# Two small steps of a two-layer encoder kernel moved: the exponent of the cumulative decays, and its negative

## The chip, the cores and the metric

The kernel runs on one core of a Trainium2 chip. The metric is device time in microseconds (us) of one execution, given as the median of several runs. The engines are named as the profile names them: PE (TensorE matmul), PEld (TensorE weight load), DVE (VectorE), ACT (ScalarE), POOL (GpSimd) and SP (SyncE, which here only issues DMAs).

## The reference, cut to what matters

Two residual layers over 256 tokens of width 1024. Each layer makes one wide projection and runs two token mixers side by side: a gated delta rule in both directions, and a differential softmax attention. The gated delta rule, in its chunked form:

```python
g = jnp.cumsum(g.reshape(bsz, nh, nc, CHUNK), axis=-1)
gdiff = g[..., :, None] - g[..., None, :]
decay = jnp.where(lower, jnp.exp(jnp.where(lower, gdiff, 0.0)), 0.0)
L = jnp.where(strict, jnp.einsum('bhncd,bhnmd->bhncm', kb, k) * decay, 0.0)
T = triangular_solve(eye + L, eye)
u, w = T @ vb, T @ (kb * jnp.exp(g)[..., None])
# per chunk, in order:
v_new = u_c - w_c @ state
o = (q_c * jnp.exp(g_c)[..., None]) @ state + qk_c @ v_new
```

What the change is about is `exp(g)`: the exponent of the cumulative log decays. In the kernel it is the tile `E_` (128 x 32: two directions by two chunks by eight heads), and `nE` is its negative. `E_` scales the second term of the output, `nE` the correction of the second chunk's values.

## The kernel before, in words

The kernel uses chunks of 128 tokens, so a layer has two per direction. All matmuls of the projections take operands split in a high and a low part (`hi_...`, `lo_...`): ACT casts the high part of a 256-row piece of weights (`weights`, line 308), DVE subtracts it from the raw weights to get the low part (line 310), and PE makes three products with them (`proj_tm`, lines 324, 325 and 326: high by high, high by low, low by high). High and low tiles have two buffers each, raw tiles three. Four such pieces make a projection; PE goes from one to the next without any other work between, so a piece that is late makes PE wait.

A layer begins with the value projections of the attention (`pp_vb`), and the k projections of the delta rule (`pf_k`), followed by the convolution of k. In `conv` each block of channels is convolved with five taps: ACT makes the middle tap out of PSUM (line 675, `cvk`, `cvq`, `cvv`), DVE adds the four others (line 679), ACT makes a tanh (line 685, `thk`, `thq`), and DVE multiplies (line 690, which for q and k writes `kq`). Then come the q projections of the delta rule (`pf_q`), in two halves, and between them the first q projection of the attention (`pp_qk`).

`gates()` is written after the k convolutions. It makes the log decays, sums them with a matmul, turns them (`gcps`), and writes `ngc`, the negative of the cumulative log decays (line 776), then `E_` with ACT's Exp (line 777) and `nE` with DVE (line 778). `log_decays()` takes the sums of squares of k, and among others their logarithm with ACT's Ln (line 742, in place on a part of the tile that order calls `ge`); `lnc` (lines 744 to 746) is made of it. `decays` raises the decay tiles `B` with ACT, `weigh_k` sums them (line 824, `dsum`) and multiplies the sum with the gram matrix of k into `A` (line 825, four times in a layer), and `turn_blocks()` comes behind it; its first step is an Exp of the small tile `kds` (line 843).

`E_` is first read by line 1015, and `nE` by line 1005, in `chunks`, long after the projections around which they are made.

The order on each engine is decided at build time: a scheduler places each instruction by what it needs and by its own estimates. `tc.high_priority(offset=HP)` lets an instruction go as early as it can, and `behind(x)` places one behind the instruction x. Ahead of some activations, where the function changes, the build puts an `ACT_TABLE_LOAD` on ACT. The program has 11 rows of that kind, before and after the change.

Of the kernel before, what the change touches and what calls it, by code (L numbers as in the profile page):

```python
# [11 lines left out]
AF = mybir.ActivationFunctionType  # L12
ALU = mybir.AluOpType
# [15 lines left out]
HP = None  # L29
# [20 lines left out]
def hybrid_encoder(  # L50
# [19 lines left out]
    V, S, G, T = nc.vector, nc.scalar, nc.gpsimd, nc.tensor  # L70
# [15 lines left out]
    def bank(name):  # L86
        return ps_m.tile([P, 512], F32, tag="m", name=name)
# [10 lines left out]
    def mid(ap, n):  # L98
        return ap.unsqueeze(1).to_broadcast([ap.shape[0], n] + list(ap.shape[1:]))
# [4 lines left out]
    mark = {}  # L104
# [44 lines left out]
    def heads4(ap):  # L149
        return ap.rearrange("p (h e) -> p h e", e=P)  # L150
# [119 lines left out]
    def behind(ins):  # L270
        return nullcontext() if ins is None else tc.issue_after(ins)
# [235 lines left out]
    for l in range(DEPTH):  # L507
# [223 lines left out]
        nE = small.tile([P, 4, NH], F32, tag="nE", name=f"nE{l}")  # L731
        ngc = small.tile([P, 4, NH], F32, tag="ngc", name=f"ngc{l}")
        E_ = small.tile([P, 4, NH], F32, tag="E_", name=f"E_{l}")

        def log_decays():
            kss = e_[:, :, 32:40]
            V.tensor_scalar(kss, ssk, 4.0 * EPS, None, ALU.add)
            kh = small.tile([P, NM, NH], F32, tag="kh", name=f"kh{l}")
            V.tensor_scalar(kh, kss, 1.0 / 16.0, None, ALU.mult)
            G.tensor_tensor(nrm.rearrange("p m h -> p (m h)"), kh.rearrange("p m h -> p (m h)"),  # L740
                            phalf, ALU.pow)
            S.activation(kss, kss, AF.Ln)
            for d in range(2):
                V.scalar_tensor_tensor(lnc[:, d], ev[:, :, d * 8 : d * 8 + 8], -1.0, kss,
                                       ALU.mult, ALU.subtract)
            V.tensor_tensor(lnc.rearrange("p d c h -> p (d c) h"), lnc.rearrange("p d c h -> p (d c) h"),
                            ngc, ALU.add)
# [6 lines left out]
        def gates():  # L754
            with behind(mark[f"k{l}1", 0][0]):
                S.activation(ev, ev, AF.Ln)
            V.scalar_tensor_tensor(ev, a_, 0.0, ev, ALU.max, ALU.add)
            glog = small.tile([P, NM, 16], F32, tag="glog", name=f"glog{l}")
            V.tensor_tensor(glog, ev[:, :, 16:32], mid(nega, NM), ALU.mult)

            gr_ps = bank(f"grps{l}")
            for d in range(2):
                for c in range(NM):
                    dc = 2 * d + c
                    T.matmul(gr_ps[0:8, dc * P : (dc + 1) * P], glog[:, c, d * 8 : d * 8 + 8],
                             tri[:, d, :], start=True, stop=True)
            grow = work.tile([8, 4, P], F32, tag="w2c", name=f"grow{l}", bufs=3)
            with behind(mark[f"k{l}1", 3][1]):
                V.tensor_copy(grow.rearrange("h c i -> h (c i)"), gr_ps[0:8, :])
            gv = gdr.rearrange("c h d i -> h d c i")  # L770
            for d in range(2):
                G.dma_start(out=gv[:, d], in_=grow[:, 2 * d : 2 * d + 2])
            gc_ps = bank(f"gcps{l}")
            for dc in range(4):
                T.transpose(gc_ps[:, dc * 8 : dc * 8 + 8], grow[:, dc, :], ident[:8, :8])
            V.tensor_scalar(ngc, gc_ps[:, :32].rearrange("p (c h) -> p c h", c=4), -1.0, None, ALU.mult)
            S.activation(E_, ngc, AF.Exp, scale=-1.0)
            V.tensor_scalar(nE, E_, -1.0, None, ALU.mult)


        A = big.tile([P, 2, NM, 4, P], F32, tag="A", name=f"A{l}")
# [3 lines left out]
        def gram(nm, g, c, slot, after=None):  # L785
            gp = (bank if slot else bank_c)(f"{nm}{l}{g}{c}")
            for j4 in range(4):
                kqh = kq[:, 4 * g + j4, c]
                with behind(after):
                    mark[nm, g, c] = T.matmul(gp[:, j4 * P : (j4 + 1) * P], kqh[:, 0, :], kqh[:, slot, :],  # L790
                                              start=True, stop=True).ins
            return heads4(gp)
# [28 lines left out]
        def weigh_k(g, c):  # L821
            dec = B[:, c, 4 * g : 4 * g + 4].rearrange("p h d i -> p d h i")
            dsum = work.tile([P, 4, P], F32, tag="w2c", name=f"dsum{l}{g}{c}", bufs=3)
            V.tensor_tensor(dsum, dec[:, 0], dec[:, 1], ALU.add)
            V.tensor_tensor(A[:, g, c], gram("kk", g, c, 0), dsum, ALU.mult)

        def weigh_q(g, c, after):
            bv = B[:, c, 4 * g : 4 * g + 4]
# [12 lines left out]

        def turn_blocks():
            S.activation(kds, kds, AF.Exp)
            Av = A.rearrange("p g c h i -> p (g c h) i")
            for b in range(4):
                G.dma_start(out=adr[b].rearrange("t j i -> j t i"), in_=Av[blk(b), :, blk(b)])
            adv = adr.rearrange("b t j i -> (b t) j i")
            G.dma_start(out=la[0:64], in_=adv)
            G.dma_start(out=lt[64:P], in_=adv)
            G.memset(X, 0.0)  # L850
            G.memset(X.rearrange("p c i -> p (c i)")[:, 0:1024:33], 1.0)
# [268 lines left out]
        with tc.high_priority(offset=HP):  # L1120
            gates()
# [7 lines left out]
        lambdas()  # L1129
        spread()  # L1130
        log_decays()
        conv("q", C_QA, 1, 0)
        qk_part(0, 0)
        cut = mark["qkT", 0]
        decays(0, 0)
        weigh_k(0, 0)
        decays(0, 1)
        weigh_k(0, 1)
        decays(1, 0)
        weigh_k(1, 0)  # L1140
        decays(1, 1)
        weigh_k(1, 1)
        turn_blocks()
        conv("q", C_QA, 1, 1)
        take_blocks()
# [237 lines left out]
```

## Time and profile before

| | |
|---|---|
| median of 3 runs | 751.39 us (750.81 to 751.85) |
| the profiled execution | 751.43 us, of which the profile spans 749.7 us |
| granted TensorE clock, mean | 0.997 |
| PE busy | 739.6 us, 99% of the span |
| PEld busy | 641.2 us, 86% |
| DVE busy | 586.4 us, 78% |
| ACT busy | 480.9 us, 64% |
| POOL busy | 139.0 us, 19% |

PE is busy nearly all of the time. A row of a timeline gives the start, the time that the instruction was busy, engine, line, operation, the tile written and the tiles read, and in brackets how long the engine had been idle and who ended it. Consecutive instructions overlap by a little, so the distance between two starts is shorter than what one is busy.

### The profile page before, as it was taken

What the parts mean: (1) busy time and instruction counts of PE and PEld (TensorE: products, weight loads), DVE (VectorE), ACT (ScalarE), POOL (GpSimd) and SP (SyncE); (2) the same over time, 40 slices, a digit from 0 to 9 for tenths busy, and PEclk for the clock granted to TensorE, in tenths of its full rate; (3) what the DMA queues carried; (4) which work ended last, traced back from release to release, by engine and by line L of the source; (5) the groups of instructions that cost most, each with busy time, mean ns of one, the idle gap of its engine ahead of it and who ended that gap; (6) DMA issues with size and microseconds to landing.
All of it is one profiled execution on the core that took longest, in us unless ns stands there. A gap on an engine that the chain in (4) does not pass through costs nothing.

```text
span 749.7 us, 13916 instructions
## 1 busy us (share of the span) xinstructions
PE 739.6 (99%) x5176; PEld 641.2 (86%) x5176; DVE 586.4 (78%) x1109; ACT 480.9 (64%) x1022; POOL 139.0 (19%) x221
## 2 busy tenths in 40 slices
PE   8999999999999999999999999999999999999996
PEld 6999899987888889888889889889778888998885
DVE  8696898999985965578667769999999669537782
ACT  6657775667876576645456578555787757566552
POOL 5004111112022440100000150202110425301000
PEclk9999999999999999999999999999999999999998
DMA  8755566776666462567674466767666747336641
GB/s 260 238 169 169 167 171 199 212 209 198 208 182 177 151 181 84 170 199 245 202 232 134 130 189 174 216 178 233 199 171 194 197 129 234 94 114 200 218 143 57
DMA packets 73734, 135.46 MB, mean 181 GB/s; under 512 B 12944, under 2 KB 13921, under 8 KB 73666
## 3 DMA queue, kind: packets, MB, share of 16 engines
q1 hardware_dynamic: 64750, 113.65, 50.3%
q0 software_dynamic: 7936, 19.35, 8.8%
q10 hardware_dynamic: 980, 1.58, 0.6%
q8 instruction: 41, 0.67, 0.4%
q14 instruction: 27, 0.22, 0.1%
HBM read 125.53 MB, written 9.01 MB: 179 GB/s over the span
## 4 chain that ended last, share of the span: by engine, by line
PE 95%; DVE 1%; issue 1%; ACT 1%; DMA 1%; SPq 0%; POOLq 0%; POOL 0%; DVEq 0%; ACTq 0%
PE pp_vb L369 4%; PE pp_qk L325 4%; PE pp_qk L326 3%; PE pp_qk L324 3%; PE sc L1060 2%; PE pp_o L369 2%; PE pf_k L385 2%; PE pp_za L325 2%; PE pf_v L385 2%; PE pf_v L389 2%; PE pp_gb L324 2%; PE pp_gb L325 2%; PE pp_zb L324 2%; PE pf_q L387 2%; PE pf_k L387 2%; PE pf_v L387 2%
## 5 line engine op out<-in xcount | busy, mean ns | idle before, releaser
L325 PE MATMUL pp_qk<-lo_qk,hT 128*128 128x512 f32 x128 | 50.5, 395 | 1.1 <-DVE lo_qk L310 1.1
L326 PE MATMUL pp_qk<-hi_qk,hT 128*128 128x512 f32 x128 | 49.9, 390 | 0.0
L310 DVE TENSOR_TENSOR lo_qk<-raw_qk,hi_qk 128x1024 fp32r<-128x1024 f32 x32 | 39.0, 1220 | 11.8 <-ACT hi_qk L308 11.6
L324 PE MATMUL pp_qk<-hi_qk,hT 128*128 128x512 f32 x128 | 45.4, 395 | 0.0
L308 ACT CAST hi_qk<-raw_qk 128x1024 fp32r<-128x1024 f32 x28 | 29.4, 1049 | 22.9 <-PE pp_qk L326 7.1
L1070 ACT ACTIVATE es<-sc,mx 128x256 f32<-128x256 f32 x64 | 29.6, 474 | 19.6 <-DVE mx L1068 19.6
L310 DVE TENSOR_TENSOR lo_pb<-raw_pb,hi_pb 128x1024 fp32r<-128x1024 f32 x16 | 19.6, 1224 | 21.2 <-ACT hi_pb L308 20.9
L387 PE MATMUL pf_q<-hT,hi_q 128*128 128x256 f32 x128 | 36.1, 286 | 0.0
L385 PE MATMUL pf_k<-hT,hi_k 128*128 128x256 f32 x128 | 36.0, 287 | 0.0
L385 PE MATMUL pf_v<-hT,hi_v 128*128 128x256 f32 x128 | 35.8, 285 | 0.0
L387 PE MATMUL pf_v<-hT,hi_v 128*128 128x256 f32 x128 | 35.8, 284 | 0.0
L385 PE MATMUL pf_q<-hT,hi_q 128*128 128x256 f32 x128 | 35.8, 284 | 0.0
L387 PE MATMUL pf_k<-hT,hi_k 128*128 128x256 f32 x128 | 35.7, 283 | 0.0
L389 PE MATMUL pf_q<-hT,lo_q 128*128 128x256 f32 x128 | 35.1, 287 | 0.0
L389 PE MATMUL pf_v<-hT,lo_v 128*128 128x256 f32 x128 | 34.5, 287 | 0.0
L389 PE MATMUL pf_k<-hT,lo_k 128*128 128x256 f32 x128 | 34.3, 283 | 0.0
L308 ACT CAST hi_pa<-raw_pa 128x1024 fp32r<-128x1024 f32 x16 | 16.9, 1055 | 22.2 <-PE pp_pa L326 16.0
L679 DVE SCALAR_TENSOR_TENSOR cvq<-pf_q,cw,cvq 128x254 f32<-128x254 f32 (+1 forms) x64 | 29.9, 477 | 0.9 <-ACT cvq L675 0.2
L325 PEld LDWEIGHTS pp_qk<-lo_qk,hT 128*128 128x128 f32 x128 | 24.0, 188 | 7.4 <-DVE lo_qk L310 2.4
L679 DVE SCALAR_TENSOR_TENSOR cvv<-pf_v,cw,cvv 128x254 f32<-128x254 f32 (+1 forms) x64 | 29.7, 474 | 0.1
L679 DVE SCALAR_TENSOR_TENSOR cvk<-pf_k,cw,cvk 128x254 f32<-128x254 f32 (+1 forms) x64 | 29.0, 477 | 1.0 <-ACT cvk L675 0.2
L310 DVE TENSOR_TENSOR lo_pa<-raw_pa,hi_pa 128x1024 fp32r<-128x1024 f32 x16 | 19.6, 1224 | 11.2 <-ACT hi_pa L308 11.2
(414 smaller groups left out, 2536.9 us busy)
## 6 DMA issues: line engine op xcount, KB each, us to landing
raw_qk<-in_w_in_dram SPq DMA_DIRECT2D x32, 512.0 KB, 3.8
raw_k<-in_w_in_dram SPq DMA_DIRECT2D x16, 512.0 KB, 4.5
raw_q<-in_w_in_dram SPq DMA_DIRECT2D x16, 512.0 KB, 3.7
raw_v<-in_w_in_dram SPq DMA_DIRECT2D x16, 512.0 KB, 3.8
raw_zb<-in_w_in_dram SPq DMA_DIRECT2D x16, 512.0 KB, 3.7
raw_za<-in_w_in_dram SPq DMA_DIRECT2D x16, 512.0 KB, 3.7
raw_ga<-in_w_in_dram SPq DMA_DIRECT2D x16, 512.0 KB, 4.7
raw_pb<-in_w_pb_dram SPq DMA_DIRECT2D x16, 512.0 KB, 3.9
```

What stands on the lines that cost most here:

```text
L308: high = (V.tensor_copy if kp in turned else S.copy)(hi[:, :, :n], raw[:, :, :n]).ins
L310: mark[nm, kp] = high, V.tensor_tensor(lo[:, :, :n], raw[:, :, :n], hi[:, :, :n].bitcast(F32), ALU.subtract).ins
L324: T.matmul(o, act[kt // 4][:, 0, kt % 4, ts_], hi, start=kt == 0, stop=False)
L325: T.matmul(o, act[kt // 4][:, 0, kt % 4, ts_], lo, start=False, stop=False)
L326: mark["proj"] = T.matmul(o, act[kt // 4][:, 1, kt % 4, ts_], hi, start=False, stop=kt == KT - 1).ins
L369: mark["proj"] = T.matmul(o, act[kt // 4][:, pa, kt % 4, ts_], ws[kt][1 + pw], start=kt == 0 and n_ == 0, stop=kt == KT - 1 and n_ == 2).ins
L385: T.matmul(o, hi[:, cs], act[kt // 4][:, 0, kt % 4, :], start=first, stop=False, skip_group_check=True)
L387: T.matmul(o, hi[:, cs], act[kt // 4][:, 1, kt % 4, :], start=False, stop=False, skip_group_check=True)
L389: T.matmul(o, lo[:, cs], act[kt // 4][:, 0, kt % 4, :], start=False, stop=done, skip_group_check=True)
L679: V.scalar_tensor_tensor(ca[:, o0:o1], acc[:, b, o0 + sft : o1 + sft], cw[:, j, cb : cb + 1], ca[:, o0:o1], ALU.mult, ALU.add)
L1060: mm = T.matmul(sp[n][:, qt * SEQ : (qt + 1) * SEQ], qkT[h // 4][rows, 0, h % 4, qt * P : (qt + 1) * P], qkT[h // 4][rows, 1, h % 4, :], s ...
L1070: S.activation(es[:, n, qt, :], spv[:, qt, :], AF.Exp, bias=mx[:, n, qt : qt + 1], accum_out=s_all[:, h, n, qt : qt + 1])
```

## The change

Two edits. The Exp that makes `E_` leaves `gates()` and is written in `log_decays()`, right behind the Ln of the k norms, and tied to it. The negation that makes `nE` leaves `gates()` too and is tied behind the last of the four products that write `A`. No instruction is added or taken away, and no value changes.

```diff
@@ log_decays
-            S.activation(kss, kss, AF.Ln)
+            with behind(S.activation(kss, kss, AF.Ln).ins), tc.high_priority(offset=HP):
+                S.activation(E_, ngc, AF.Exp, scale=-1.0)
@@ gates
             V.tensor_scalar(ngc, gc_ps[:, :32].rearrange("p (c h) -> p c h", c=4), -1.0, None, ALU.mult)
-            S.activation(E_, ngc, AF.Exp, scale=-1.0)
-            V.tensor_scalar(nE, E_, -1.0, None, ALU.mult)
@@ weigh_k
-            V.tensor_tensor(A[:, g, c], gram("kk", g, c, 0), dsum, ALU.mult)
+            mark["A"] = V.tensor_tensor(A[:, g, c], gram("kk", g, c, 0), dsum, ALU.mult).ins
@@ turn_blocks
             S.activation(kds, kds, AF.Exp)
+            with behind(mark["A"]):
+                V.tensor_scalar(nE, E_, -1.0, None, ALU.mult)
```

In the rows of order that follow, the line numbers are each program's own: from line 743 to 776 the changed one is one line further, and from line 779 to 842 it is one line back. What a row waits for stands in brackets; the numbers behind the names tell buffers and semaphores apart.

ACT, first layer, around the Ln of the k norms (`ge`), before. `thq` is the tanh of the first block of the q convolution, `hi_qk` are the high parts of the attention's first q projection:

```order
L308 CAST hi_qk_1044<-raw_qk_1046 128x1024 [waits DMAHW6_49,DVE_49,PE_49]
L742 ACT_TABLE_LOAD
L742 ACTIVATE ge_347<-ge_347 128x2x8 [waits DVE_49]
L685 ACT_TABLE_LOAD [waits DVE_49]
L685 ACTIVATE thq_996<-cvq_990 128x256 [waits Activation_49]
L675 ACTIVATE cvq_999<-pf_q_868,cw_300 128x256
L308 CAST hi_qk_1062<-raw_qk_1064 128x1024 [waits DMAHW7_49,PE_49]
```

The same place in the changed program:

```order
L308 CAST hi_qk_1043<-raw_qk_1045 128x1024 [waits DMAHW6_49,DVE_49,PE_49]
L742 ACT_TABLE_LOAD
L742 ACTIVATE ge_347<-ge_347 128x2x8 [waits DVE_49]
L743 ACT_TABLE_LOAD
L743 ACTIVATE E_369<-ngc_368 128x32
L685 ACTIVATE thq_995<-cvq_989 128x256 [waits DVE_49,Activation_49]
L675 ACTIVATE cvq_998<-pf_q_867,cw_300 128x256
L308 CAST hi_qk_1061<-raw_qk_1063 128x1024 [waits DMAHW7_49,PE_49]
```

`E_` now stands between the Ln and the tanh. The second table load, which stood ahead of the tanh and held its wait for DVE, stands ahead of `E_` and waits for nothing; the wait for DVE has gone over to the tanh. In the second layer the same rows stand in the same order.

DVE, first layer, the old place of `nE`, before:

```order
L776 TENSOR_SCALAR ngc_368<-gcps_754 128x32 [waits PE_49]
L679 SCALAR_TENSOR_TENSOR cvk_538<-pf_k_390,cw_300,cvk_538 128x254 [waits DVE_49]
L310 TENSOR_TENSOR lo_q_901<-raw_q_902,hi_q_900 128x1024 [waits DMAHW2_49,Activation_49]
L778 TENSOR_SCALAR nE_367<-E_369 128x32 [waits Activation_49]
L690 SCALAR_TENSOR_TENSOR kq_359<-thk_544,cvk_538 128x2x128 [waits Activation_49]
L679 SCALAR_TENSOR_TENSOR cvk_547<-pf_k_390,cw_300,cvk_547 128x254 [waits Activation_49]
```

DVE, first layer, its new place, in the changed program:

```order
L823 TENSOR_TENSOR dsum_1183<-B_371 128x512 [waits DMASW6_49,Activation_49,Pool_49]
L679 SCALAR_TENSOR_TENSOR cvq_1323<-pf_q_1201,cw_300,cvq_1323 128x254 [waits Activation_49]
L824 TENSOR_TENSOR A_370<-kk_1185,dsum_1183 128x512 [waits DVE_49,PE_49]
L844 TENSOR_SCALAR nE_367<-E_369 128x32
L310 TENSOR_TENSOR lo_qk_1397<-raw_qk_1398,hi_qk_1396 128x1024 [waits DMAHW7_49,Activation_49]
L679 SCALAR_TENSOR_TENSOR cvq_1323<-pf_q_1201,cw_300,cvq_1323 128x255 [waits DVE_49] x2
```

`nE` has gone from between a low part and a multiplication of the k convolution to behind the last product into `A`, ahead of a low part of the attention's second q projection, and its wait for ACT is gone. In the second layer it moves between the same two stages.

PE, second layer, the beginning of the q projection of the delta rule, before. `ctk` are transposes of convolved k:

```order
L385 MATMUL pf_q_4814<-hT_0_4047,hi_q_4816 128x256 [waits Activation_49]
L387 MATMUL pf_q_4814<-hT_0_4047,hi_q_4816 128x256
L389 MATMUL pf_q_4814<-hT_0_4047,lo_q_4817 128x256
L706 MATMUL ctk_4650<-ident,kq_4305 128x128 [waits DVE_49]
L706 MATMUL ctk_4650<-ident,kq_4305 128x128
```

The same place in the changed program:

```order
L385 MATMUL pf_q_4813<-hT_0_4047,hi_q_4815 128x256 [waits Activation_49]
L387 MATMUL pf_q_4813<-hT_0_4047,hi_q_4815 128x256
L706 MATMUL ctk_4650<-ident,kq_4305 128x128 [waits DVE_49]
L706 MATMUL ctk_4650<-ident,kq_4305 128x128
L389 MATMUL pf_q_4813<-hT_0_4047,lo_q_4816 128x256
```

Two transposes have changed places with one matmul. Nothing else moves: PE of the first layer, POOL and SP keep their order.

## The prediction

> **What bounds the kernel now.** I read the page's head first, then PE's waits, then the stretch around the longest wait that the change can reach: the chain, then ACT, DVE and PE in order of time. The head and the whole list of PE's waits:
>
> ```profile
> span 749.7 us, 13916 instructions
> PE 739.6 (99%) x5176; PEld 641.2 (86%) x5176; DVE 586.4 (78%) x1109; ACT 480.9 (64%) x1022; POOL 139.0 (19%) x221
> PE idle L410 <- DVE ones L407: 1.1, 1, 1.1
> PE pp_qk L325 <- DVE lo_qk L310: 1.1, 2, 0.5
> PE pp_vb L464 <- ACT wktm_vb L308: 0.8, 1, 0.8
> PE pp_vb L464 <- ACT hT L234: 0.3, 1, 0.3
> PE pt_h L227 <- DVE h_n L216: 0.2, 1, 0.2
> ```
>
> PE is the bound. Only what removes a wait of PE can shorten the run, and there are few. Four of the five rows belong to the opening or a norm; the second is the low part of the attention's first q projection, once in each layer. No row names `pf_k`, `ctk`, L369 or `pf_q`, the work around the old places of `E_` and `nE`: what is saved there is hidden under PE. The chain in the first layer, in order of time, runs through that second row:
>
> ```profile
> 78.50 1.18 issue
> ...
> 81.43 1.24 DVE lo_qk L310
> 82.71 0.50 PE pp_qk L325
> ```
>
> The 1.18 us of "issue" lie on ACT, ahead of the tanh. ACT's own rows say what it is, in the first layer and in the second:
>
> ```profile
> 75.05 1.05 ACT L308 CAST hi_qk<-raw_qk 128x1024 fp32r<-128x1024 f32 x1
> 76.11 1.28 ACT L742 ACT_TABLE_LOAD   x1
> 77.41 0.22 ACT L742 ACTIVATE ge<-ge 128x16 f32<-128x16 f32 x1
> 78.38 1.28 ACT L685 ACT_TABLE_LOAD   x1 [0.76 <-DVE cvq L679]
> 79.68 0.42 ACT L685 ACTIVATE thq<-cvq 128x256 f32<-128x256 f32 x1
> 80.00 0.46 ACT L675 ACTIVATE cvq<-pf_q,cw 128x256 f32<-128x256 f32 x1
> 80.36 1.04 ACT L308 CAST hi_qk<-raw_qk 128x1024 fp32r<-128x1024 f32 x1
> ...
> 443.92 0.22 ACT L742 ACTIVATE ge<-ge 128x16 f32<-128x16 f32 x1
> 444.90 1.28 ACT L685 ACT_TABLE_LOAD   x1 [0.76 <-DVE cvq L679]
> 446.20 0.42 ACT L685 ACTIVATE thq<-cvq 128x256 f32<-128x256 f32 x1
> ```
>
> It is a table load. The load needs no data, but it carries the tanh's wait for DVE's convolution: ACT stands idle for 0.76 us, and only then loads for 1.28 us. Behind the tanh, DVE waits as long, and the low part that PE needs is queued behind:
>
> ```profile
> 80.13 0.42 DVE L690 SCALAR_TENSOR_TENSOR kq<-thq,cvq 128x256 f32<-128x256 f32 x1 [1.72 <-ACT thq L685]
> ```
>
> How much PE loses there is read from its own starts:
>
> ```profile
> 76.56 0.39 PE L326 MATMUL pp_qk<-hi_qk,hT 128*128 128x512 f32 x1
> ...
> 80.87 0.39 PE L325 MATMUL pp_qk<-lo_qk,hT 128*128 128x512 f32 x1
> 81.10 0.39 PE L326 MATMUL pp_qk<-hi_qk,hT 128*128 128x512 f32 x1
> 81.45 0.73 PE L324 MATMUL pp_qk<-hi_qk,hT 128*128 128x512 f32 x2
> 82.71 0.50 PE L325 MATMUL pp_qk<-lo_qk,hT 128*128 128x512 f32 x1 [0.52 <-DVE lo_qk L310]
> ...
> 87.63 0.39 PE L326 MATMUL pp_qk<-hi_qk,hT 128*128 128x512 f32 x1
> ...
> 447.62 0.39 PE L326 MATMUL pp_qk<-hi_qk,hT 128*128 128x512 f32 x1
> 449.23 0.50 PE L325 MATMUL pp_qk<-lo_qk,hT 128*128 128x512 f32 x1 [0.53 <-DVE lo_qk L310]
> ```
>
> From 80.87 to 81.10 is one step, 0.23 us. Three steps behind 81.10 the first low-part product was due at 81.79; it started at 82.71, 0.92 us late. In the second layer, 447.62 plus 0.69 gives 448.31 against 449.23: again 0.92. So the list's 0.5 understates it, since the pair of L324 ahead of it also started late. Both layers together hold 1.84 us.
>
> **The change part by part.** *The Exp, new place.* The table load moves with the wait taken off: it follows the Ln at once. The Ln ends at 77.41 + 0.22 = 77.63. The load ahead of the Ln started 0.01 us behind the cast that ended at 76.10, and the Ln 0.02 behind the load's end, so the new load runs from 77.64 to 78.92 and `E_` starts at 78.94. What `E_` takes of ACT's time is the distance to its successor in the old place:
>
> ```profile
> 50.67 0.22 ACT L777 ACTIVATE E<-ngc 128x32 f32<-128x32 f32 x1
> 50.80 0.42 ACT L685 ACTIVATE thk<-cvk 128x256 f32<-128x256 f32 x1
> ```
>
> That is 0.13 us; its input is ready long before. The tanh can start at 78.94 + 0.13 = 79.07. Its data were there when the old load was let go, at 78.38, so it waits for nothing. Against 79.68 this is 0.61 us earlier. The same sum in the second layer: 443.92 + 0.22 + 0.01 + 1.28 + 0.02 + 0.13 = 445.58 against 446.20, so 0.62.
>
> Does PE get all of it? DVE's `kq`, its two taps and the low part follow one another without a gap in ACT's wake, and the cast of `hi_qk` at 80.36 also stands right behind ACT's tanh and tap. The cast must also find its buffer free and its raw weights landed. Its buffer is the first piece's, whose last product stands twelve steps of 0.23 before the second piece's last at 81.10, at 78.3 plus its 0.39: free well before the new 79.75. The weights:
>
> ```profile
> 68.19 6.72 SPq L304 DMA_DIRECT2D raw_qk<-in_w_in_dram  x3
> ...
> raw_qk<-in_w_in_dram SPq DMA_DIRECT2D x32, 512.0 KB, 3.8
> ```
>
> The last of these three issues was over at 74.91, and 3.8 us later, at 78.7, it has landed. So the whole chain moves by 0.61: high part ready at 80.79, and L325 starts at 82.10, where it was due at 81.79. About 0.31 us of the wait stays, still held by the low part. Were the cast held after all, the gain would be zero; that is the lower bound, and the 0.92 of the wait the upper one. I take 0.61, since each row of the chain stands right behind the one before.
>
> At this place a rule of the Trainium skill (ScalarE: Activation LUTs, section "Table sets: the hidden batching unit") speaks against the change: Ln and Exp share a set, so an Exp behind an Ln needs no load. By it the load would stay with the tanh behind the wait, and the sum would be no gain but twice the 0.13 of `E_` lost; the changed program's order, with a load row between the Ln and `E_`, says otherwise.
>
> *The Exp and the negation, old places.* ACT gets 0.13 us back, DVE the `nE` row and in the second layer a wait for `E_`:
>
> ```profile
> 51.94 0.17 DVE L778 TENSOR_SCALAR nE<-E 128x32 f32<-128x32 f32 x1
> ...
> 419.34 0.18 DVE L778 TENSOR_SCALAR nE<-E 128x32 f32<-128x32 f32 x1 [0.27 <-ACT E L777]
> ```
>
> At most 0.17 us in the first layer and 0.45 in the second. PE waits for nothing there, so I count zero; the bounds are zero and 0.62 us, were PE's work paced by DVE in a way its list doesn't show.
>
> *The negation, new place.* It stands ahead of a low part; behind it are queued that and the convolution's taps.
>
> ```profile
> 105.58 1.22 DVE L310 TENSOR_TENSOR lo_qk<-raw_qk,hi_qk 128x1024 fp32r<-128x1024 f32 x1
> ...
> 107.97 0.39 PE L325 MATMUL pp_qk<-lo_qk,hT 128*128 128x512 f32 x1
> ```
>
> The low part is done at 106.80 and PE first uses it at 107.97: 1.17 us of cover for at most 0.17. Cost zero; without the cover, 0.17 a layer.
>
> *The two transposes of the second layer.* They go one matmul earlier; they wait for a `kq` of DVE.
>
> ```profile
> 427.61 0.42 DVE L690 SCALAR_TENSOR_TENSOR kq<-thk,cvk 128x256 f32<-128x256 f32 x1
> 428.49 0.28 PE L389 MATMUL pf_q<-hT,lo_q 128*128 128x256 f32 x1
> 428.60 0.38 PE L706 MATMUL ctk<-ident,kq 128*128 128x128 f32 x2
> ```
>
> `kq` is done at 428.03, the new start is 428.49: 0.46 us to spare. Cost zero. Both readers of `E_` and `nE` come a hundred microseconds later in the program, in `chunks`.
>
> **The sum.** 0.61 + 0.62 = 1.23 us. From the profiled execution's 751.43 (span 749.7 and 1.73 around it) that gives 750.20; the median of the runs, 751.39, is 0.04 lower, which gives 750.16. I say 750.2, a gain of 0.16%. A measurement of this kernel tells about 0.2% (1.5 us) from no change, so the likeliest case falls inside "the same".
>
> **The rivals.**
>
> *More than the head start.* Behind the late start, the 21 steps from 82.71 to 87.63 take 4.92 us, 0.234 each, against 0.227 over the 20 steps from 76.56 to 81.10; if that slowness belongs to the wait, a shorter wait saves up to 0.15 us a layer more, and 749.9. At the far end the whole wait goes: 751.4 - 1.84 = 749.5. For it: the same slowness in both layers. Against it: the low part stays in DVE's queue, and 0.31 remain by the sum. Chance 0.15.
>
> *The gain is given back.* PE gets to a later piece earlier, and there waits for something that did not move, a transfer or POOL. Then 751.4, or something between that and 750.6. For it: weights come through the SP queue one after another. Against it: PE's waits show no row from here to the layer's end, and ACT and DVE move along. Chance 0.12.
>
> *Slower: the load does not run behind the Ln at once.* If ACT must be empty before a load starts, the old place got that for nothing, in its 0.76 us of idling, and the new one pays it. It decides from 0.61 us on. Priced with as much as a load itself, 1.28, the tanh would start at 80.35, 0.67 late, and PE in its wake: 1.34 us for both layers, 752.7; the range of this case goes to 753. Against it: the load at 76.11 started 0.01 us behind a cast that had been running for 1.05 us. Chance 0.05. The Trainium skill (ScalarE: Activation LUTs, section "What ACT_TABLE_LOAD costs") has this rule: a switch of sets takes 1283 ns and a drain of about 1380 ns. The trace agrees on the first with 1.28 us, and shows no drain ahead of the load at 76.11.
>
> *It moves nothing.* The load at the new place could prove to serve Exp alone, the tanh needing one more. The changed order shows none. Chance 0.02, price as the last one's.
>
> **How the numbers follow.** The forecast has 0.66, with a range of its own from 749.8 to 750.7 (the runs of before lie within 0.6 us of their median). 749.5 to 751.3 takes in the rival of more, and most of the one given back. Faster by over 0.2%, below 749.9: most of the rival of more, and a tenth of the forecast's own spread, 0.20. Slower by over 0.2%: about half of the slower cases and some unnamed, 0.05. The same: 0.75.
>
> **What would show it.** On ACT, right behind the Ln and without idle time, a load of 1.28 us, `E_`, and a tanh that starts about 1.66 us behind the Ln's start instead of 2.27. DVE's wait for `thq` falls from 1.72 to about 1.1 us, in both layers. PE's wait for `lo_qk` at L325 stays as a row, with the start about 0.3 us late instead of 0.92. The load rows stay as many. Wrong would be: idle time or a drain ahead of the load, a further load ahead of the tanh, a PE wait at `ctk`, or all steps right and the end not earlier, with new waits of PE in the later stages.

## The result, and the profile after

The changed kernel takes 750.34 us (median of 22 runs), the kernel before, run beside it, 751.41 us (22 runs). The ratio is 0.9984, with a 95% interval from 0.9978 to 0.9991. The interval is that of a gain between 0.7 and 1.7 us. The profiled execution took 750.29 us with a span of 748.5 us, against 751.43 and 749.7 before. Of all executions reported here and below one is of a slow kind, 1483.31 us in the first series with the tiny Exp, and it is left out of that ratio.

The whole list of PE's waits, after:

```profile
PE idle L410 <- DVE ones L407: 1.1, 1, 1.1
PE pp_vb L464 <- ACT hT L234: 0.6, 1, 0.6
PE pp_vb L464 <- ACT wktm_vb L308: 0.3, 1, 0.3
PE pp_vb L464 <- DVE wktm_vb L310: 0.2, 1, 0.2
```

The row of `lo_qk` is gone, the only one of PE's waits that lay outside the opening and the norm; so is the 0.2 us of `pt_h`, and the three rows of `pp_vb`, all in the opening, sum to 1.1 us as the two did before. ACT around the Ln, in the first layer and in the second:

```profile
76.13 1.28 ACT L742 ACT_TABLE_LOAD   x1
77.43 0.22 ACT L742 ACTIVATE ge<-ge 128x16 f32<-128x16 f32 x1
77.66 1.28 ACT L743 ACT_TABLE_LOAD   x1
78.95 0.23 ACT L743 ACTIVATE E<-ngc 128x32 f32<-128x32 f32 x1
79.09 0.40 ACT L685 ACTIVATE thq<-cvq 128x256 f32<-128x256 f32 x1
...
443.32 0.22 ACT L742 ACTIVATE ge<-ge 128x16 f32<-128x16 f32 x1
443.56 1.28 ACT L743 ACT_TABLE_LOAD   x1
444.85 0.23 ACT L743 ACTIVATE E<-ngc 128x32 f32<-128x32 f32 x1
444.99 0.40 ACT L685 ACTIVATE thq<-cvq 128x256 f32<-128x256 f32 x1
```

The load follows the Ln at once, and the tanh `thq` starts 1.66 us behind the Ln's start (79.09 - 77.43), and 1.67 in the second layer; before it was 2.27 and 2.28. DVE's wait for it, and PE's starts:

```profile
79.52 0.43 DVE L690 SCALAR_TENSOR_TENSOR kq<-thq,cvq 128x256 f32<-128x256 f32 x1 [1.09 <-ACT thq L685]
...
81.12 0.39 PE L326 MATMUL pp_qk<-hi_qk,hT 128*128 128x512 f32 x1
81.35 0.61 PE L324 MATMUL pp_qk<-hi_qk,hT 128*128 128x512 f32 x2
82.10 0.50 PE L325 MATMUL pp_qk<-lo_qk,hT 128*128 128x512 f32 x1
82.44 0.40 PE L326 MATMUL pp_qk<-hi_qk,hT 128*128 128x512 f32 x1
...
87.02 0.39 PE L326 MATMUL pp_qk<-hi_qk,hT 128*128 128x512 f32 x1
...
447.02 0.39 PE L326 MATMUL pp_qk<-hi_qk,hT 128*128 128x512 f32 x1
447.25 0.61 PE L324 MATMUL pp_qk<-hi_qk,hT 128*128 128x512 f32 x2
448.01 0.50 PE L325 MATMUL pp_qk<-lo_qk,hT 128*128 128x512 f32 x1
448.35 0.40 PE L326 MATMUL pp_qk<-hi_qk,hT 128*128 128x512 f32 x1
...
452.99 0.39 PE L326 MATMUL pp_qk<-hi_qk,hT 128*128 128x512 f32 x1
```

Three steps of 0.23 behind 81.12, L325 was due at 81.81; it started at 82.10, 0.29 us late. In the second layer: due 447.71, started 448.01, 0.30 late. Before, it was 0.92 in both. PE thus gained 0.63 and 0.62 us at the two places, 1.25 together, and the span is 1.2 us shorter: the gain is made here, and as far as the span shows none of it is lost further on.

### The profile page after: what moved, and what is told of

It reads as the page before. It is cut to its first block, busy times and chain, and to the rows that moved or that the text cites. A ratio compares the mean times of both kernels' runs of the same rounds, so it can differ in the third digit from the quotient of the medians.

```text
span 748.5 us, 13917 instructions
## 1 busy us (share of the span) xinstructions
PE 739.3 (99%) x5176; PEld 641.7 (86%) x5176; DVE 586.5 (78%) x1109; ACT 481.2 (64%) x1022; POOL 139.5 (19%) x221
## 4 chain that ended last, share of the span: by engine, by line
PE 95%; ACT 2%; issue 1%; DVE 1%; DMA 1%; SPq 0%; POOLq 0%; POOL 0%; DVEq 0%; ACTq 0%
PE pp_vb L369 4%; PE pp_qk L325 4%; PE pp_qk L326 3%; PE pp_qk L324 3%; PE sc L1061 2%; PE pp_o L369 2%; PE pf_k L385 2%; PE pp_za L325 2%; PE pf_v L385 2%; PE pf_v L389 2%; PE pp_gb L324 2%; PE pp_gb L325 2%; PE pp_zb L324 2%; PE pf_q L387 2%; PE pf_k L387 2%; PE pf_v L387 2%
## 5 line engine op out<-in xcount | busy, mean ns | idle before, releaser
L325 PE MATMUL pp_qk<-lo_qk,hT 128*128 128x512 f32 x128 | 50.5, 395 | 0.3
L324 PE MATMUL pp_qk<-hi_qk,hT 128*128 128x512 f32 x128 | 45.1, 393 | 0.0
L325 PEld LDWEIGHTS pp_qk<-lo_qk,hT 128*128 128x128 f32 x128 | 24.0, 188 | 6.6 <-DVE lo_qk L310 1.6
```

The costliest lines, as they stand in the source:

```text
L324: T.matmul(o, act[kt // 4][:, 0, kt % 4, ts_], hi, start=kt == 0, stop=False)
L325: T.matmul(o, act[kt // 4][:, 0, kt % 4, ts_], lo, start=False, stop=False)
```

## The experiments

Theory A, that of the prediction: what gains is that the table load no longer stands behind the tanh's wait for DVE. Theory B: the gain comes from the slots that `E_` and `nE` leave free in the k stage. A third theory gives it to the order of two transposes in the second layer. In every experiment the kernel before ran beside, on the same chip, and the ratios are to it. The line numbers in their rows are each kernel's own.

**A tiny Exp instead of the move.** `E_` and `nE` stay where they were; an Exp of one constant per partition stands behind the Ln. What it writes is read by nobody. The code is cut: the tile `tiny` (128 x 1) is made at the start of the kernel, here and further down.

```diff
-            S.activation(kss, kss, AF.Ln)
+            with behind(S.activation(kss, kss, AF.Ln).ins), tc.high_priority(offset=HP):
+                S.activation(tiny, phalf[:, :1], AF.Exp)
```

> The kernel before, with E_ and nE in their old places, and one more Exp of a single constant per partition tied behind the Ln. Theory A, the load is taken out from behind the tanh's wait: the load follows the Ln at once, the tanh thq starts about 1.65 us behind the Ln's start (2.27 before), PE's low-part product L325 is about 0.3 us late instead of 0.92 in each layer, and the time is 750.2 +- 0.3. Theory B, the gain comes from the slots that E_ and nE leave free in the k stage: nothing is freed here, an Exp is added, and the time is 751.4 or a little above.

The first series gave 750.05 us, ratio 0.9976 (0.9967 to 0.9985), and no profile that can be set beside the others. The second series of the same kernel:

> The kernel before with one more Exp of a constant behind the Ln, E_ and nE in their old places, once more, for its profile. Theory A: on ACT the load starts at once behind the Ln, the tanh starts about 1.60 to 1.66 us behind the Ln's start, L325 is about 0.3 us late in both layers, and the time is that of the change, 750.1 to 750.4. Theory B: 751.4.

This gave 750.15 us, ratio 0.9982 (0.9973 to 0.9991), and ACT in the first layer:

```profile
76.94 0.21 ACT L743 ACTIVATE ge<-ge 128x16 f32<-128x16 f32 x1
77.17 1.28 ACT L744 ACT_TABLE_LOAD   x1
78.47 0.20 ACT L744 ACTIVATE tiny<-phalf 128x1 f32<-128x1 f32 x1
78.58 0.40 ACT L686 ACTIVATE thq<-cvq 128x256 f32<-128x256 f32 x1
```

The tanh starts 1.64 us behind the Ln's start, as in the change, and PE's low-part product is 0.26 us late in the first layer and 0.27 in the second. Nothing was freed in the k stage, and the gain is all there: theory B falls. The order of PE, too, is that of the kernel before (in the second layer the first two transposes start at 427.49, behind the low-part product of `pf_q` at 427.37), so the third theory falls with it.

**The negation alone.** `nE` goes behind the last product into `A`, `E_` stays in `gates()`. The code is cut: `mark["A"]` is set as in the change.

```diff
@@ gates
-            V.tensor_scalar(nE, E_, -1.0, None, ALU.mult)
@@ turn_blocks
+            with behind(mark["A"]):
+                V.tensor_scalar(nE, E_, -1.0, None, ALU.mult)
```

> The kernel before, with nE alone tied behind the last product into A; E_ stays where it was. Theory A: the load stays behind the tanh's wait, L325 starts 0.92 us late in both layers as before, 751.4 +- 0.3. Theory B: DVE gets its 0.17 and 0.45 us back as in the change, and half or more of the gain is seen, 750.6 to 750.9.

It gave 751.41 us, ratio 0.9997 (0.9988 to 1.0005), no change. PE waits as before:

```profile
82.73 0.50 PE L325 MATMUL pp_qk<-lo_qk,hT 128*128 128x512 f32 x1 [0.52 <-DVE lo_qk L310]
```

What DVE gets back in the k stage is worth nothing, and neither does `nE` ahead of the low part of the second q projection cost anything.

**The second layer alone.** In the first layer `E_`'s Exp stays in `gates()`; that part of the code is cut here.

```diff
+            ln = S.activation(kss, kss, AF.Ln).ins
+            if l:
+                with behind(ln), tc.high_priority(offset=HP):
+                    S.activation(E_, ngc, AF.Exp, scale=-1.0)
```

> The change in the second layer only; the first layer has E_'s Exp in its old place. Theory A (the load is taken out from behind the tanh's wait, once in each layer): half of the gain, 750.8 +- 0.3; L325 is 0.92 us late in the first layer and about 0.31 late in the second. Theory B (PE's order of two transposes in the second layer, which this kernel shares with the change, is what gains): all of the gain, 750.3.

It gave 750.6 us, ratio 0.9989 (0.998 to 0.9997). In the first layer L325 starts 0.91 us late (due 81.78, started 82.69), in the second 0.29 (due 448.34, started 448.63):

```profile
82.69 0.50 PE L325 MATMUL pp_qk<-lo_qk,hT 128*128 128x512 f32 x1 [0.53 <-DVE lo_qk L310]
...
448.63 0.50 PE L325 MATMUL pp_qk<-lo_qk,hT 128*128 128x512 f32 x1
```

The interval of the ratio holds both a half and the whole of the gain, and by itself it tells little; the starts of PE tell that each layer has its own share.

**Three copies between `E_` and the tanh.** They write a tile that nobody reads.

```diff
-                S.activation(E_, ngc, AF.Exp, scale=-1.0)
+                last_ = S.activation(E_, ngc, AF.Exp, scale=-1.0).ins
+            for _ in range(3):
+                with behind(last_), tc.high_priority(offset=HP):
+                    last_ = S.copy(sqj, ident).ins
```

> The change, with three copies of a 128x128 tile put on ACT between E_ and the tanh; what they write is read by nobody. Theory A: the tanh's start sets PE's start one for one, so three copies at about 0.2 us each put the tanh at about 79.7 in the first layer, L325 0.9 us late again in both layers, and the time at 751.4 +- 0.3, as before the change. A theory by which the tanh's start does not matter says 750.3.

It gave 751.96 us, ratio 1.0005 (0.9996 to 1.0014): the gain is gone. ACT, and then PE, in the first layer:

```profile
79.13 0.94 ACT L746 COPY sqj<-ident 128x128 f32<-128x128 f32 x3
79.98 0.41 ACT L685 ACTIVATE thq<-cvq 128x256 f32<-128x256 f32 x1
...
81.16 0.39 PE L326 MATMUL pp_qk<-hi_qk,hT 128*128 128x512 f32 x1
81.74 0.73 PE L324 MATMUL pp_qk<-hi_qk,hT 128*128 128x512 f32 x2 [0.19 <-ACT hi_qk L308]
83.00 0.50 PE L325 MATMUL pp_qk<-lo_qk,hT 128*128 128x512 f32 x1 [0.53 <-DVE lo_qk L310]
```

The copies took 0.28 us each from start to start, not 0.2, so the tanh came 0.89 us later than in the change (79.98 against 79.09). L325 was due at 81.85 and is 1.15 late, 0.86 more than in the change. Twice 0.86 is 1.72 us; the span is 750.2 against 748.5, 1.7 more. The tanh's start sets PE's start nearly one for one.

**The negation behind `lnc`.** `nE` stands behind the tap that the tanh waits for, in DVE's wait for the tanh, and no longer behind `A`.

```diff
+            end = V.tensor_tensor(lnc.rearrange("p d c h -> p (d c) h"), ..., ngc, ALU.add).ins
+            with behind(end):
+                V.tensor_scalar(nE, E_, -1.0, None, ALU.mult)
```

> The change, with nE tied on DVE behind the last step of lnc, that is behind the tap that the tanh waits for and ahead of the wait for the tanh, instead of behind the products into A. All engines but DVE have the order of the change. Theory A: DVE waits for the tanh there anyway, so nE costs nothing: 750.3 +- 0.3, the tanh at 79.1. If being out of the way of E_ needs the place behind A, or if nE's row ahead of the low part of the second q projection counts, this run differs from the change by 0.3 us or more.

It gave 750.16 us, ratio 0.9985 (0.9977 to 0.9994), as the change. The tie behind `A` is not needed for the gain.

**The negation right behind `E_`.** The same, but `nE` is tied to `E_` and may go as early as it can.

```diff
+                mark["E"] = S.activation(E_, ngc, AF.Exp, scale=-1.0).ins
+            with behind(mark["E"]), tc.high_priority(offset=HP):
+                V.tensor_scalar(nE, E_, -1.0, None, ALU.mult)
```

> The change, with nE not behind the products into A but right behind E_. Theory A: where nE stands matters nothing, DVE waits for the tanh there anyway: 750.3 +- 0.3, L325 about 0.3 us late. Theory B: DVE still has nE out of the k stage, 750.3 too, so this run does not tell A from B; it tells whether the tie behind A has a share of its own. If nE between A and the low part costs or gains anything, this run differs from the change by up to 0.3 us.

This expectation was wrong: 754.09 us, ratio 1.0034 (1.0023 to 1.0046), 2.5 us slower than before. DVE and ACT in the first layer:

```profile
77.74 0.25 DVE L747 SCALAR_TENSOR_TENSOR lnc<-ge 128x16 f32<-128x16 f32 x2
79.28 0.18 DVE L745 TENSOR_SCALAR nE<-E 128x32 f32<-128x32 f32 x1 [1.28 <-ACT E L743]
79.37 0.48 DVE L679 SCALAR_TENSOR_TENSOR cvq<-pf_q,cw,cvq 128x254 f32<-128x254 f32 x1
...
79.94 0.42 ACT L685 ACTIVATE thq<-cvq 128x256 f32<-128x256 f32 x1 [0.69 <-DVE lnc L749]
```

The scheduler put `nE` ahead of the last tap that the tanh needs. DVE waits 1.28 us for `E_`, the tap stands behind that wait, and the tanh behind the tap: it starts at 79.94, later than before the change, and L325 is 1.10 us late in both layers. Against the change that is 0.81 and 0.80, 1.6 of the 3.75 us between the two medians. The scheduler also ordered PE's work of the following projections otherwise, and PE's waits have a new row, that of a later projection, `pp_zb`:

```profile
PE pp_zb L325 <- DVE lo_zb L310: 1.1, 2, 0.5
```

Most of the rest is lost there: from the first product of `pp_zb` to the first of the projection behind it, `pp_za`, PE takes 29.53 us in the first layer and 29.39 in the second, and 28.29 and 28.32 after the change, 2.3 us more together. Why the low part is late there was not taken apart.

**The Ln's load out of the chain as well.** The change, with an Ln of a constant where ACT sat idle for 2.2 us, after the fourth cast of the q projection's weights.

```diff
         conv("q", C_QA, 1, 0)
+        with behind(mark[f"q{l}0", 3][0]), tc.high_priority(offset=HP):
+            S.activation(tiny, phalf[:, :1], AF.Ln)
```

> The change, and one more Ln of a single constant tied behind the cast of the q projection's fourth weight piece, where ACT sat idle for 2.2 us; the Ln of the k norms then needs no load of its own. Theory A: the one load that stays in the chain ends before the convolution that the tanh waits for, thq starts at about 78.4 in the first layer, L325 starts on its due step in both layers, and the time is 749.7 +- 0.3, 0.6 below the change. If the slow steps behind the wait (0.234 us against 0.227) belong to the wait, they go too, and the time is 749.4. Theory B: nothing is freed in the k stage, and the time is that of the change, 750.3.

It gave 749.22 us, ratio 0.9966 (0.9954 to 0.9979), a little below both times that were expected, and was run once more:

> The change with the early Ln once more, for its interval, since it stood on few runs: 749.2 +- 0.3, about 1.1 us below the change, of which the wait of 0.31 us in each layer is 0.6 and the slow steps behind it are 0.3.

749.25 us, ratio 0.9969 (0.9957 to 0.998). ACT and PE of the first run, first layer:

```profile
68.96 1.28 ACT L1136 ACT_TABLE_LOAD   x1
70.25 0.20 ACT L1136 ACTIVATE tiny<-phalf 128x1 f32<-128x1 f32 x1
...
75.70 0.21 ACT L743 ACTIVATE ge<-ge 128x16 f32<-128x16 f32 x1
75.93 1.28 ACT L744 ACT_TABLE_LOAD   x1
77.23 0.23 ACT L744 ACTIVATE E<-ngc 128x32 f32<-128x32 f32 x1
78.10 0.42 ACT L686 ACTIVATE thq<-cvq 128x256 f32<-128x256 f32 x1 [0.65 <-DVE lnc L748]
...
80.81 0.39 PE L327 MATMUL pp_qk<-hi_qk,hT 128*128 128x512 f32 x1
81.03 0.61 PE L325 MATMUL pp_qk<-hi_qk,hT 128*128 128x512 f32 x2
81.49 0.39 PE L326 MATMUL pp_qk<-lo_qk,hT 128*128 128x512 f32 x1
...
86.25 0.39 PE L327 MATMUL pp_qk<-hi_qk,hT 128*128 128x512 f32 x1
```

Now the tanh waits for its data, and the low-part product starts on its step, three behind 80.81. This version beats both kernels. By the medians it is 1.1 us below the change; by PE's starts 1.0, of which the two waits are 0.6 and the steps behind them 0.4.

**The early Ln without the change.** The same line, in the kernel before.

> The kernel before, with one more Ln of a constant behind the cast of the q projection's fourth weight piece and nothing else: the Ln of the k norms needs no load then, but the tanh's load keeps its wait for DVE. Theory A (what counts is that a load stands behind the tanh's wait, not how much ACT loads or when it is done with the Ln): the load still starts when the convolution is done, the tanh starts where it did, L325 is 0.92 us late in both layers, and the time is 751.4 +- 0.3. A theory by which the first load's 1.28 us are worth the same as the second's says 750.2 or less.

It gave 751.38 us, ratio 0.9998 (0.9989 to 1.0007). ACT in the first layer:

```profile
75.98 0.21 ACT L743 ACTIVATE ge<-ge 128x16 f32<-128x16 f32 x1
78.37 1.28 ACT L686 ACT_TABLE_LOAD   x1 [2.18 <-DVE cvq L680]
79.66 0.42 ACT L686 ACTIVATE thq<-cvq 128x256 f32<-128x256 f32 x1
```

ACT is done with the Ln 1.4 us earlier (75.98 against 77.41), idles 2.18 us instead of 0.76, and begins the tanh's load when it always did. The same line that gains 1.1 us on top of the change gains nothing without it.

## Why the prediction was right

**The bound and the place.** Outside the opening and a norm PE waited at one place in each layer, and the chain through the table load, the tanh, DVE's taps and the low part is what set that wait. The filler shows it from the one side, the early Ln from the other.

**The sum.** Predicted were 0.61 and 0.62 us; PE's starts moved by 0.63 and 0.62, the span by 1.2, the medians by 1.07, which is 0.16 less than the sum and within the interval. The remaining wait was put at 0.31 and is 0.29 and 0.30. The time was forecast at 750.2 and is 750.34.

**The parts at nothing.** The freed slots in the k stage, `nE` behind `A` and the transposes were counted as zero, each with its cover. The negation alone (0.9997) and the tiny Exp (0.9982) agree.

**The rival of more.** The slow steps behind the wait did not shrink with it: 21 steps from 82.10 to 87.02 take 4.92 us after the change, to the hundredth what they took before, and in the second layer 4.98 (from 448.01 to 452.99) against 4.99 (from 449.23 to 454.22). Before, the rows behind those of the prediction are:

```profile
83.04 0.40 PE L326 MATMUL pp_qk<-hi_qk,hT 128*128 128x512 f32 x1
...
449.57 0.40 PE L326 MATMUL pp_qk<-hi_qk,hT 128*128 128x512 f32 x1
...
454.22 0.39 PE L326 MATMUL pp_qk<-hi_qk,hT 128*128 128x512 f32 x1
```

They show that the 0.234 us of the prediction is an average over unlike steps. The first step behind the wait took 0.33 us (82.71 to 83.04), the other 20 took 4.59, 0.229 each. Of the 0.15 us that were put down to slowness, 0.1 are that one step. In the second layer the first step took 0.34 and the others 0.232 each, so the slowness was not the same in both layers, as the prediction had it. After the change the first step took 0.34 in both. Only where the wait went altogether did all of this go too: 4.76 us from 81.49 to 86.25 with the early Ln, and 4.76 in its second layer (447.00 to 451.76). So that rival named something real, but not something that a shorter wait buys.

**The rivals of nothing and of slower.** Nothing was given back later. The load behind the Ln started 0.01 us after the Ln's end (77.66 against 77.43 + 0.22), so there is no drain to pay. The drain of about 1380 ns that the Trainium skill (ScalarE: Activation LUTs, section "What ACT_TABLE_LOAD costs") adds to a switch is not seen in the loads shown here: those that had no wait to carry begin 0.01 or 0.02 us behind the activation ahead of them, and the next activation starts 0.02 us or less behind a load's end (after the change, 77.66 + 1.28 against 78.95). The 1283 ns that the Trainium skill gives there for the load itself agree with 1.28. The shared set of Ln and Exp that the Trainium skill speaks of (ScalarE: Activation LUTs, section "Table sets: the hidden batching unit") does not spare the load either: a load stands between the two in every kernel that has them side by side here.

**What the prediction's signs got wrong.** It expected PE's wait at L325 to stay as a row, and the row went: PE's pair of L324 ahead of it runs until 81.96 (81.35 + 0.61), so PE is idle for 0.14 us only while its next start is 0.29 late. The starts showed it, the list of waits did not.

**What it left out.** It priced the place of `nE` only where the change puts it. That a late `E_` with an early `nE` would hold DVE, and through it the tanh, came out by chance, in an experiment meant to show that the place is indifferent.

## What to carry to other kernels

In these kernels a table load took over the wait of the activation ahead of which it was put. An activation of the same table that needs no waiting, placed ahead, takes the load out of the wait; it can be one that the kernel has anyway, or one of a constant. The gain is at most the part of the load that then runs during the wait: here 0.61 us of its 1.28, with the time of `E_` paid. Whoever moves a step later on one engine has to look where its reader stands on another: in the run with the negation right behind `E_`, DVE waited 1.28 us for the moved step and held all that was queued behind, even the tap that the moved step's own engine waited for.

## What the runs showed of the hardware

In these kernels a table load took 1.28 us, began 0.01 or 0.02 us behind the activation ahead of it where it had nothing to wait for (77.66 against 77.43 + 0.22 after the change), and the next activation began 0.01 or 0.02 us behind its end (78.95 against 77.66 + 1.28).

Behind a late start, PE's first step of the 128x512 products took 0.33 or 0.34 us instead of 0.227, however late the start was (0.92 or 0.29 us). The 20 steps behind it took 0.229 us each in the first layer and 0.232 in the second, before and after the change; where the start was on time, all 21 took 0.227 (4.76 us). The granted TensorE clock was 1.00 in these stretches, with the slow steps and without. In the changed kernel's trace the weights of the late product began to load only with it, at 82.10, while those of the product at 81.12 began to load at 80.90. That this is what the first step costs was not tested, and why the 20 others are slower was not found out. Slower steps are not bound to a late start: before the change the 8 from 101.81 to 103.66 took 1.85 us, 0.231 each, with no wait of PE listed there.
